# Swapped queries by transfer, the gate with w_ada's columns moving, and other buffer counts in a two-group encoder layer

## The chip, the cores and the metric

The kernel runs on one core of one Trainium2 chip, as one launch. The metric is the device time in microseconds of that core, the median of several executions. Before the change it is 2014.87 us over three runs (2009.33 to 2015.93).

The core has a matrix engine (PE; PEld is its loading of the stationary operand), a vector engine (DVE), a scalar engine for activation functions (ACT), a general engine (POOL), and a queue engine (SP), from which this kernel issues all of its transfers. Every engine and SP work through their own list of instructions in order, and a wait in one holds up what stands behind it in the same list.

## What is computed

One layer of a bidirectional encoder for two groups of 1024 tokens (width 1024), which share all weights. Reduced to what matters here:

```python
mod = silu(c) @ w_ada + b_ada                  # (1024) @ (1024 x 3072)
shift, scale, gate = split(mod, 3)
h = rms_norm(x, norm_g) * (1 + scale) + shift
qa, ka, va, za, qb, kb, vb, zb, ga, gb = split(h @ w_in)
# branch A: 8 query heads, 2 key heads, 64 wide, RMS norm and rotation of q and k
oa = softmax(qa ka^T / 8) va * silu(za)
# branch B: 4 heads, two softmax maps each, 128-wide values
ob = rms_norm((softmax1 - lam * softmax2) vb) * (1 - lam_init) * silu(zb)
merged = sigmoid(ga) * (oa @ w_proj_a) + sigmoid(gb) * (ob @ w_proj_b)
y = x + gate * (merged @ w_out)
```

All data is float32. Most products are made of two halves of each operand, a rounded one (type fp32r) and the remainder, in three matmuls (high x high, high x low, low x high).

## The kernel before

**Tiling.** Everything is cut into 128 partitions. A group's `h` lies transposed in eight large buffers (`u`, 8 KB a partition; pool `upool`, 16 buffers). Keys, queries, values, merged products and the start's inputs use the same pool. Weights come in pieces of 256 columns (`load_w`): four transfers into staging tiles `st` (3 buffers), ACT rounds each (L177), POOL or DVE makes the remainder (L179).

**Queries and keys.** `qa_gen` and `qkb_gen` compute 256 columns for 128 tokens at a time (`proj_tt`, L488). `rms` then takes the mean square (ACT copy and square, DVE sum L504, POOL scaling and addition of EPS L505, POOL power L506), POOL multiplies and rotates (L508 to L528; in the phases where attention does not run, DVE does every second one), PE transposes (L539), and ACT and DVE write the high and low half of a query or key into the two halves of a tile's partitions (L541, L542): high on 0 to 63 and low on 64 to 127, or the other way round.

**Scores.** A unit of attention is one head with 256 queries (two times 128, t = 0 and 1), so 32 units in branch A and 16 in branch B per group; a unit of B has two maps. `softmax_unit` makes 128 x 1024 scores in a PSUM bank `s` (two of them): queries times keys (L697), then the same queries with their partition halves exchanged, `sw`, times the same keys (L698), which gives the four products of the halves in two passes. DVE takes the maximum (L699), ACT the exponential into a tile `p` of probabilities (L700; pool `ppool`, 3 buffers). In B, DVE combines both maps (L733). `flip` transposes on DVE in blocks of 32 (L734) and moves four quarters by transfer into `q`, a tile for the whole unit (L739; two buffers). The values' matmuls then use `q` (L759, L760 in A, L799 in B).

**The swap.** `swapped` copies the halves for 128 queries on POOL, 64 partitions by 128 columns at a time (L565): two instructions for a unit half in A, four in B. It runs one step ahead within a phase: the second half's when the first half's scores are issued, the next unit's when the second half's are. `sw` has two buffers.

**The gate.** `gate_gen` computes the residual's gate for both groups, in group 0's last phase of attention. The stationary operand is a block of w_ada with 128 columns, and the two conditioning vectors move, so a matmul has two columns (L435): 64 matmuls, each a float32 one. At the start, `ada` computes shift and scale the other way round: the two vectors are stationary and 512 columns of w_ada move (L298), and four small transposes turn the row into columns (L307). `inv_rms` (L271) has matmuls that move one column of ones.

**What sets the order.** Streams of generators are woven with shares (`weave`): attention, the making of queries and keys, and the z pieces (`z_gen`, L667; each ends with ACT's copy into the one buffer `ev`, L673, and a store). How many z pieces fall to which phase, and how early each stream runs, is given by the tables at the top (`Z_SHARE`, `ATT_W`, `IN_A` and so on). A scheduler then orders the instructions of each engine, with the attention's at a raised priority. The last phases gate the branches' outputs (`gated_gen`, L895 with a SiLU on ACT), project and merge (`merge_gen`, L940, L951) and project out (`out_gen`, L969).

Of the kernel before, what the change touches and what calls it, by code (L numbers as in the profile page):

```python
# [38 lines left out]
    (7, 18, 4, 3, 5, 6),  # L39
)  # L40
Z_HEAD = (5, 3)
Z_HEAD_A = (-0.35, -0.25)
ATT_W = (
    (1.0, 0.9, 1.1, 0.95, 1.0, 1.322),
    (1.15, 1.265, 0.9, 1.0, 0.85, 1.069),
)
IN_A = (
    (0.1, 0.05, 0.2, 0.05, 0.15, 0.1),
    (0.1, 0.05, 0.45, 0.1, 0.15, 0.55),
# [3 lines left out]
    (0.15, 0.05, 0.35, 0.05, 0.0, -0.1),  # L53
)
LAST_ATT, LAST_FILL = (44, 32)
GATED_A = -0.1
TAIL = 6
TAIL_A = 0.3
LAG = 2

# [28 lines left out]
def kernel(ctx: ExitStack, tc: tile.TileContext, t: dict):  # L89
# [336 lines left out]
    def gate_gen():  # L426
        for n in range(NCH):
            ps = gbank()[:, :2]
            for q in range(2):
                st = spool.tile([P, 4, P], F32, tag="st", name=nm("st"))  # L430
                col = 2 * D + n * P
                dma(st, w_ada[q * 512 : (q + 1) * 512, col : col + P].rearrange("(c p) n -> p c n", p=P))
                for c in range(4):
                    k = q * 4 + c
                    nc.tensor.matmul(ps, st[:, c], cT[:, k], start=(k == 0), stop=(k == NCH - 1))  # L435
            nc.vector.tensor_scalar(out=gatec[:, n], in0=ps, scalar1=bcol[:, 2, n : n + 1], scalar2=None, op0=ALU.add)
            yield 1
# [58 lines left out]
    def rms(ps, nh, e):  # L496
        n = nh * HD
        row = rtile()
        raw, sq = row[:, :n], row[:, 256 : 256 + n]
        nc.scalar.activation(raw, ps, AF.Copy)  # L500
        nc.scalar.activation(sq, raw, AF.Square)
        ss = tiny.tile([P, 4], F32, tag="ss", name=nm("ss"))[:, :nh]
        rs = tiny.tile([P, 4], F32, tag="rs", name=nm("rs"))[:, :nh]
        nc.vector.tensor_reduce(out=ss, in_=sq.rearrange("p (h d) -> p h d", d=HD), axis=AX.X, op=ALU.add)  # L504
        nc.gpsimd.tensor_scalar(out=ss, in0=ss, scalar1=1.0 / HD, scalar2=EPS, op0=ALU.mult, op1=ALU.add)  # L505
# [52 lines left out]
    def swapped(u, qt):  # L558

        qs = u["q"]  # L560
        sw = mtile("sw", [P, 2, P], F32R)[:, : len(qs)]
        sl = slice(qt * P, (qt + 1) * P)
        for m, q in enumerate(qs):
            for a, b in ((LO, HI), (HI, LO)):
                nc.gpsimd.tensor_scalar(  # L565
                    out=sw[a, m], in0=q[b, sl].bitcast(F32), scalar1=1.0, scalar2=1.0, op0=ALU.mult, op1=ALU.mult
                )
        return sw

# [26 lines left out]
    def qa_gen(st, half):  # L596
# [12 lines left out]
        def back(tt, x3):  # L609
            sl = slice(tt * P, (tt + 1) * P)  # L610
            pairs_T(x3, qs[0][:, :, sl], qs[1][:, :, sl])

        yield from pipelined(ht, w, front, back)

    def qkb_gen(ht, out, h):
# [11 lines left out]
        def back(tt, x3):  # L627
            sl = slice(tt * P, (tt + 1) * P)
            pairs_T(x3, qk[0][:, :, sl], qk[1][:, :, sl])

# [25 lines left out]
    def z_gen(ht, col, dst, i0):  # L656
        w = load_w(w_cols(w_in, (col, 256)))
        for hf in range(2):
            for e in range(2):
# [13 lines left out]
                nc.scalar.activation(ev, ps, AF.Copy)  # L673
# [31 lines left out]
    def scores(u, i):  # L705
# [8 lines left out]
        softmax_unit(u["q"][m][:, qt * P : (qt + 1) * P], u["sw"][:, m], u["k"][m], pt, su)  # L714
        if m == 0:
            u[t] = [pt]
            u.pop("next", None)
# [114 lines left out]
    def attention(units):  # L832
# [3 lines left out]
        for n, (ph, make) in enumerate(units):  # L836
# [7 lines left out]
        for at, ph, n, i, qk in steps:  # L844
# [4 lines left out]
            with tc.high_priority(offset=AHEAD):  # L849
# [24 lines left out]
    def gated_gen(st, i, hf, oT):  # L874
# [15 lines left out]
        for c in range(2):  # L890
# [4 lines left out]
            nc.scalar.activation(z, z, AF.Silu)  # L895
# [109 lines left out]
    def units_of(st):  # L1005
# [17 lines left out]

        units = []
        for half in range(2):
            units += [(half, lambda a=(half, i, pr): a_unit(*a)) for i in (0, 2, 1, 3) for pr in range(4)]
        for h in range(4):
            units += [(2 + h, lambda a=(h, pr): b_unit(*a)) for pr in range(4)]
# [9 lines left out]
    def z_item(st, i):  # L1038
        ht = st["ht"]
        if i < 2:  # L1040
            return z_gen(ht, C_ZA + i * 256, st["zd"], i * 2)
        if i < 4:
            return z_gen(ht, C_ZB + (i - 2) * 256, st["zd"], i * 2)
# [118 lines left out]
```

## Time and profile before

| | |
|---|---|
| median of the runs | 2014.87 us |
| the profiled execution | 2017.56 us |
| its span, first to last instruction | 2015.8 us |
| instructions in its records | 31269 |
| transfers' bytes | 278.35 MB, a mean of 138 GB/s |
| transfers of probabilities (q<-p) | 768, each 128 KB, 2.6 us to landing |

The page of the profile gives, in this order: each engine's busy time and share of the span; the span in 40 slices of about 50 us, a digit for each (tenths busy, and in the row PEclk tenths of full clock granted to PE); the transfers' queues; the chain of work that ended last; groups of instructions by line, with total and mean duration and with the idle time ahead of them. In names such as `q<-p` the written tile stands first. A view of waits lists, for each line, how long its engine stood idle before it and whose work ended that. Matmuls overlap in the pipeline, so durations of matmuls add up to more than their stretch.

### The profile page before, as it was taken

The numbers are of one execution on the slowest core, as the hardware profiler recorded it, in microseconds if no ns is written. First come the engines' busy times: TensorE is split into PE (matmuls) and PEld (weight loads), VectorE is DVE, ScalarE is ACT, GpSimd is POOL, SyncE is SP. The second block draws the span as 40 slices with busy tenths as digits, with TensorE's granted clock in tenths as the row PEclk, the third lists the DMA queues.
The fourth block names the chain that finished last, engine by engine and source line by source line (L and its number), as shares of the span: only waits on it lengthen the run. The fifth ranks groups of instructions, "written<-read, shape, count | busy, mean of one in ns | idle before, by whom it ended". The sixth has DMA issues, their size and how long they took to land.

```text
span 2015.8 us, 31269 instructions
## 1 busy us (share of the span) xinstructions
PE 1924.6 (95%) x10554; PEld 1650.9 (82%) x10554; DVE 1305.9 (65%) x1798; ACT 1029.6 (51%) x1956; POOL 963.1 (48%) x1640
## 2 busy tenths in 40 slices
PE   8889999999999999889998899999999999998999
PEld 3778888888978988768888787888887888876887
DVE  4557766776787476546464778667777746664741
ACT  4445655565554345754323556566665434587420
POOL 2475723564677471331235675246577837522210
PEclk9999999999999996999998899999999999999999
DMA  8124545555443327754650345464544323565531
GB/s 306 48 71 109 147 139 137 148 150 154 109 125 95 90 81 206 223 191 160 208 188 32 99 123 152 137 169 126 157 127 126 88 74 90 160 212 192 183 119 73
DMA packets 255199, 278.35 MB, mean 138 GB/s; under 512 B 31680, under 2 KB 205888, under 8 KB 255040
## 3 DMA queue, kind: packets, MB, share of 16 engines
q1 hardware_dynamic: 255040, 276.36, 46.2%
q8 instruction: 84, 1.38, 0.3%
q14 instruction: 75, 0.61, 0.1%
HBM read 133.59 MB, written 42.01 MB: 87 GB/s over the span
## 4 chain that ended last, share of the span: by engine, by line
PE 58%; DVE 10%; DMA 10%; POOL 7%; ACT 6%; issue 5%; SPq 3%; ACTq 0%; POOLq 0%; DVEq 0%
PE f L667 15%; PE f L488 14%; PE f L969 4%; PE s L697 4%; PE s L698 4%; PE s L969 3%; DMA q<-p 3%; PE a L799 3%; DMA p<-zd 2%; PE a L759 2%; PE a L760 2%; SPq L739 2%; DVE m L699 2%; PE f L940 2%; ACT p L700 2%
## 5 line engine op out<-in xcount | busy, mean ns | idle before, releaser
L667 PE MATMUL f<-u,w 128*128 128x512 f32 x2208 | 580.6, 399 | 0.0
L488 PE MATMUL f<-w,u 128*128 128x256 f32 x3456 | 492.2, 288 | 2.8 <-ACT row L500 1.6
L488 PEld LDWEIGHTS f<-w,u 128*128 128x128 f32 x3456 | 464.1, 193 | 24.0 <-ACT row L500 2.7
L667 PEld LDWEIGHTS f<-u,w 128*128 128x128 f32 x2208 | 405.1, 191 | 76.0 <-ACT w L177 0.5
L700 ACT ACTIVATE p<-s,m 128x1024 f32<-128x1024 f32 x256 | 284.7, 1112 | 247.0 <-DMA q<-p 124.6
L699 DVE TENSOR_REDUCE m<-s 128x1 f32<-128x1024 f32 x256 | 310.3, 1217 | 71.6 <-PE s L698 68.2
L179 POOL TENSOR_TENSOR w<-st,w 128x512 fp32r<-128x512 f32 x168 | 231.9, 1396 | 238.7 <-ACT w L177 172.1
L565 POOL TENSOR_SCALAR sw<-u 64x128 fp32r<-64x128 f32 x520 | 180.4, 347 | 307.6 <-PE s L698 264.5
L734 DVE STREAM_TRANSPOSE p<-p 128x1024 f32<-128x1024 f32 x192 | 238.2, 1241 | 114.5 <-ACT p L700 109.2
L748 DVE TENSOR_TENSOR q<-q,hi 128x512 fp32r<-128x512 f32 x256 | 197.4, 790 | 55.0 <-ACT hi L747 53.0
L698 PE MATMUL s<-u,sw 128*128 128x512 f32 x512 | 209.1, 409 | 0.0
L747 ACT ACTIVATE hi<-q 128x512 fp32r<-128x512 f32 x256 | 153.5, 625 | 92.0 <-DMA q<-p 50.0
L177 ACT ACTIVATE w<-st 128x512 fp32r<-128x512 f32 x196 | 113.9, 625 | 93.9 <-DMA st<-in_w_in_dram 39.2
L940 PE MATMUL f<-u,w 128*128 128x512 f32 x564 | 143.5, 405 | 14.3 <-ACT ev L673 7.6
L940 PEld LDWEIGHTS f<-u,w 128*128 128x128 f32 x564 | 107.4, 193 | 39.6 <-DVE u L951 9.2
L759 PE MATMUL a<-hi,u 128*128 128x256 f32 x512 | 131.4, 283 | 5.0 <-DVE oo L776 5.0
L799 PE MATMUL a<-q,u 128*128 128x256 f32 x512 | 132.4, 395 | 1.4 <-issue 1.2
L760 PE MATMUL a<-q,u 128*128 128x256 f32 x512 | 128.6, 285 | 0.6 <-DVE q L748 0.6
L697 PE MATMUL s<-u 128*128 128x512 f32 x256 | 112.4, 440 | 16.5 <-ACT p L700 16.2
L506 POOL TENSOR_TENSOR rs<-ss,nhalf 128x4 f32<-128x4 f32 (+1 forms) x112 | 111.9, 999 | 7.4
L733 DVE SCALAR_TENSOR_TENSOR p<-p,r,p 128x1024 f32<-128x1024 f32 x64 | 91.8, 1434 | 35.2 <-POOL r L721 33.2
L697 PE MATMUL s<-u,u 128*128 128x512 f32 x256 | 104.6, 408 | 10.0 <-ACT p L700 9.7
(176 smaller groups left out, 2713.8 us busy)
## 6 DMA issues: line engine op xcount, KB each, us to landing
q<-p SPq DMA_DIRECT2D x768, 128.0 KB, 2.6
st<-in_w_in_dram SPq DMA_DIRECT2D x132, 256.0 KB, 3.1
zd<-ev SPq DMA_DIRECT2D x96, 256.0 KB, 2.4
p<-zd SPq DMA_DIRECT2D x64, 256.0 KB, 3.1
u<-in_w_ada_dram SPq DMA_DIRECT2D x8, 1024.0 KB, 10.4
st<-in_w_in_dram SPq DMA_DIRECT2D x64, 128.0 KB, 3.1
st<-in_w_out_dram SPq DMA_DIRECT2D x32, 256.0 KB, 3.0
row<-od SPq DMA_DIRECT2D x24, 256.0 KB, 3.3
```

Source lines behind the costliest of these rows:

```text
L179: e.tensor_tensor(out=wl, in0=st, in1=wh.bitcast(F32), op=ALU.subtract)
L488: nc.tensor.matmul(ps, lt[c][:, sl], w[:, c, wi, :], start=(k == 0), stop=(k == 23))
L565: nc.gpsimd.tensor_scalar(out=sw[a, m], in0=q[b, sl].bitcast(F32), scalar1=1.0, scalar2=1.0, op0=ALU.mult, op1=ALU.mult)
L667: nc.tensor.matmul(ps, w[:, c, wi, e * P : (e + 1) * P], rt[c], start=(k == 0), stop=(k == 23),)
L697: nc.tensor.matmul(s[:, sl], q, k[:, sl], start=True, stop=False)
L698: nc.tensor.matmul(s[:, sl], sw, k[:, sl], start=False, stop=True)
L699: nc.vector.tensor_reduce(out=m, in_=s, axis=AX.X, op=ALU.max, negate=True)
L700: nc.scalar.activation(pt.rearrange("p (j c a) -> p j c a", j=4, c=8), s.rearrange("p (c a j) -> p j c a", c=8, j=4), AF.Exp, bias=m, accu ...
L734: nc.vector.transpose(pt, pt)
L748: nc.vector.tensor_tensor(out=tl, in0=tl.bitcast(F32), in1=th.bitcast(F32), op=ALU.subtract)
L799: nc.tensor.matmul(acc, u["v"][:, k], pT[:, k], start=(k == 0), stop=(k == 7))
L940: nc.tensor.matmul(ps, w[:, c, wi, d * P : (d + 1) * P], o[:, oi, :], start=(k == 0), stop=(k == 11))
```

## The change

Five things are changed.

1. `swapped` makes the exchanged halves with two (A) or four (B) transfers of 64 partitions by 256 columns from SP, for the whole unit at once. They are issued behind the flip of the unit's predecessor's first half, if the queries are already there (`made` counts the token tiles that have been written), over a phase's end too; otherwise when the unit begins. `sw` has twice the columns.
2. `gate_gen` is written as `ada` is: the two vectors stationary, 512 columns of w_ada moving, 16 matmuls in place of 64, then eight small transposes.
3. In `rms`, ACT's square takes the factor 1/64 in, and the addition of EPS is DVE's instead of POOL's.
4. The large pool has 15 buffers instead of 16, the probabilities' 4 instead of 3.
5. The tables' numbers are set anew. (The new constant `SILU` is 0, which leaves every SiLU where it was.)

In the built program, PE has 64 matmuls of two columns fewer and 16 of 512 more (and eight transposes), POOL has 520 copies and 112 scalings fewer, DVE 112 additions more, SP 256 transfers more (1502 before, 1758 now), and ACT 41 table loads in place of 58.

```diff
 Z_SHARE = (
     (7, 20, 5, 3, 2, 5),
-    (7, 18, 4, 3, 5, 6),
+    (7, 18, 4, 2, 5, 6),
 )
...
-LAST_ATT, LAST_FILL = (44, 32)
+LAST_ATT, LAST_FILL = (48, 28)
...
-    upool = ent(tc.tile_pool(name="upool", bufs=16))
+    upool = ent(tc.tile_pool(name="upool", bufs=15))
...
-    ppool = ent(tc.tile_pool(name="ppool", bufs=3))
+    ppool = ent(tc.tile_pool(name="ppool", bufs=4))
...
     def gate_gen():
-        for n in range(NCH):
-            ps = gbank()[:, :2]
-            for q in range(2):
-                st = spool.tile([P, 4, P], F32, tag="st", name=nm("st"))
-                col = 2 * D + n * P
-                dma(st, w_ada[q * 512 : (q + 1) * 512, col : col + P].rearrange("(c p) n -> p c n", p=P))
-                for c in range(4):
-                    k = q * 4 + c
-                    nc.tensor.matmul(ps, st[:, c], cT[:, k], start=(k == 0), stop=(k == NCH - 1))
-            nc.vector.tensor_scalar(out=gatec[:, n], in0=ps, scalar1=bcol[:, 2, n : n + 1], scalar2=None, op0=ALU.add)
-            yield 1
+        for half in range(2):
+            acc = gbank()[:2]
+            for k in range(NCH):
+                st = spool.tile([P, 512], F32, tag="st", name=nm("st"))
+                col = 2 * D + half * 512
+                dma(st, w_ada[k * P : (k + 1) * P, col : col + 512])
+                nc.tensor.matmul(acc, cT[:, k], st, start=(k == 0), stop=(k == NCH - 1))
+                if k % 2:
+                    yield 1
+            row = rtile()[:2]
+            nc.vector.tensor_copy(row, acc)
+            ps = gbank()[:, :8].rearrange("p (c g) -> p c g", g=2)
+            for c in range(4):
+                nc.tensor.transpose(ps[:, c, :], row[:, c * P : (c + 1) * P], ident[:2, :2])
...
-        nc.scalar.activation(sq, raw, AF.Square)
+        nc.scalar.activation(sq, raw, AF.Square, scale=1.0 / math.sqrt(HD))
...
-        nc.gpsimd.tensor_scalar(out=ss, in0=ss, scalar1=1.0 / HD, scalar2=EPS, op0=ALU.mult, op1=ALU.add)
+        nc.vector.tensor_scalar(out=ss, in0=ss, scalar1=EPS, scalar2=None, op0=ALU.add)
...
-    def swapped(u, qt):
+    def swapped(u):
 
         qs = u["q"]
-        sw = mtile("sw", [P, 2, P], F32R)[:, : len(qs)]
-        sl = slice(qt * P, (qt + 1) * P)
+        sw = mtile("sw", [P, 2, 256], F32R)[:, : len(qs)]
+        sl = slice(u["pr"] * 256, u["pr"] * 256 + 256)
         for m, q in enumerate(qs):
             for a, b in ((LO, HI), (HI, LO)):
-                nc.gpsimd.tensor_scalar(
-                    out=sw[a, m], in0=q[b, sl].bitcast(F32), scalar1=1.0, scalar2=1.0, op0=ALU.mult, op1=ALU.mult
-                )
+                dma(sw[a, m].bitcast(F32), q[b, sl].bitcast(F32))
         return sw
...
-        if m == 0:
-            u["sw"] = u["next"] if "next" in u else swapped(u, qt)
+        if "sw" not in u:
+            u["sw"] = swapped(u)
...
-                    if t == 0:
-                        late.append(lambda u=live[n]: u.update(next=swapped(u, u["pr"] * 2 + 1)))
-                    elif n + 1 < len(units) and units[n + 1][0] == ph:
+                    if t == (0 if ph < 2 else 0) and n + 1 < len(units) and units[n + 1][2]():
                         live[n + 1] = units[n + 1][1]()
-                        late.append(lambda u=live[n + 1]: u.update(next=swapped(u, u["pr"] * 2)))
+                        late.append(lambda u=live[n + 1]: u.update(sw=swapped(u)))
...
+        def there(kind, n, pr):
+            return made.get(id(st[kind].get(n)), 0) > 2 * pr + 1
```

Three places show how the order moves. The names' numbers tell tiles apart; `x2` at a row's end is a repetition. First POOL, before the change, in branch B, where one head's queries are made while another's scores run: the mean square (L505, L506), multiplications and rotation (L508 to L528), the combining factor (L721), and the swaps (L565).

```order
L565 TENSOR_SCALAR sw_6499<-u_5509 64x128 x2
L565 TENSOR_SCALAR sw_6499<-u_5510 64x128 x2
L721 TENSOR_SCALAR r_6353<-r_6353,suB_118,nlam 128x1
L505 TENSOR_SCALAR ss_6477<-ss_6477 128x4
L506 TENSOR_TENSOR rs_6478<-ss_6477,nhalf 128x4
L508 TENSOR_TENSOR row_6474<-row_6474,rs_6478 128x256
L623 TENSOR_TENSOR row_6474<-row_6474,gB 128x256
L519 TENSOR_TENSOR rc_6484<-row_6474,cosB 128x4x16
L527 TENSOR_TENSOR row_6474<-row_6474,sinB 128x4x8 x2
L565 TENSOR_SCALAR sw_6591<-u_5509 64x128 x2
L565 TENSOR_SCALAR sw_6591<-u_5510 64x128 x2
L528 TENSOR_TENSOR row_6474<-rc_6484,row_6474 128x4x16
```

The same chain on POOL with the change (lines are numbered about ten higher: L515 is the power, L537 the rotation's last step):

```order
L515 TENSOR_TENSOR rs_5550<-ss_5549,nhalf 128x4
L517 TENSOR_TENSOR row_5546<-row_5546,rs_5550 128x256
L634 TENSOR_TENSOR row_5546<-row_5546,gB 128x256
L528 TENSOR_TENSOR rc_5556<-row_5546,cosB 128x4x16
L536 TENSOR_TENSOR row_5546<-row_5546,sinB 128x4x8 x2
L537 TENSOR_TENSOR row_5546<-rc_5556,row_5546 128x4x16
```

The swaps between the steps are gone, and so is the scaling ahead of the power. Second SP with the change, in branch A of group 0: flips (L750), stores of a unit's result (L791) and of a z piece (L688), and the swaps (L574).

```order
L750 DMA q_1996<-p_1954 128x1x256 x4
L791 DMA od_122<-oo_2009 64x256
L750 DMA q_1996<-p_2044 128x1x256 x4
L574 DMA sw_2321<-u_928 64x256 x2
L688 DMA zd_2463<-ev_2461 128x512
L750 DMA q_2108<-p_2085 128x1x256 x4
L750 DMA q_2108<-p_2138 128x1x256 x3
L791 DMA od_123<-oo_2130 64x256
L750 DMA q_2108<-p_2138 128x1x256
L574 DMA sw_2434<-u_928 64x256 x2
```

Two transfers now stand behind each unit's flips. The tile `sw_2321` is for the unit whose flips write `q_2429`; the flips of three other units (`q_2108`, `q_2221`, `q_2316`) stand between. Third PE in group 0's last phase, before the change, at the gate's first matmuls (L435), with scores of branch B (L697, L698) and values (L799):

```order
L435 MATMUL f_8314<-cT,st_8315 128x2 x4
L435 MATMUL f_8314<-cT,st_8321 128x2 x4
L435 MATMUL f_8333<-cT,st_8334 128x2 x4
L697 MATMUL s_8307<-u_7503 128x512
L698 MATMUL s_8307<-u_7503,sw_8300 128x512
L435 MATMUL f_8333<-cT,st_8340 128x2 x4
L697 MATMUL s_8350<-u_7504 128x512
L698 MATMUL s_8350<-u_7504,sw_8300 128x512
L799 MATMUL a_8390<-q_8243,u_7032 128x256 x8
```

And with the change (the gate is L435 again, scores are L709 and L710):

```order
L435 MATMUL f_8152<-st_8167,cT 2x512
L435 MATMUL f_8152<-st_8199,cT 2x512
L435 MATMUL f_8152<-st_8202,cT 2x512
L709 MATMUL s_8208<-u_7420 128x512
L710 MATMUL s_8208<-u_7420,sw_8077 128x512
L709 MATMUL s_8208<-u_7420 128x512
L710 MATMUL s_8208<-u_7420,sw_8077 128x512
L709 MATMUL s_8243<-u_7421 128x512
L710 MATMUL s_8243<-u_7421,sw_8077 128x512
L709 MATMUL s_8243<-u_7421 128x512
L710 MATMUL s_8243<-u_7421,sw_8077 128x512
```

Groups of four matmuls of two columns have become single ones of 512, and four passes of scores stand between two of them.

More of the change, by code (lines that the diff above doesn't have):

```diff
@@ L38 @@
     (7, 20, 5, 3, 2, 5),
-    (7, 18, 4, 3, 5, 6),
+    (7, 18, 4, 2, 5, 6),
 )
-Z_HEAD = (5, 3)
+Z_HEAD = (5, 4)
 Z_HEAD_A = (-0.35, -0.25)
 ATT_W = (
-    (1.0, 0.9, 1.1, 0.95, 1.0, 1.322),
-    (1.15, 1.265, 0.9, 1.0, 0.85, 1.069),
+    (1.0, 0.9, 1.1, 0.95, 1.0, 1.52),
+    (1.229, 1.265, 0.9, 1.0, 0.85, 1.069),
 )
 IN_A = (
-    (0.1, 0.05, 0.2, 0.05, 0.15, 0.1),
-    (0.1, 0.05, 0.45, 0.1, 0.15, 0.55),
+    (0.1, 0.05, 0.4, 0.05, -0.05, 0.1),
+    (0.1, 0.05, 0.4, 0.1, 0.15, 0.55),
 )
@@ L52 @@
     (0.15, 0.0, 0.2, -0.1, 0.0, 0.0),
-    (0.15, 0.05, 0.35, 0.05, 0.0, -0.1),
+    (0.2, 0.05, 0.35, 0.05, 0.0, -0.1),
 )
-LAST_ATT, LAST_FILL = (44, 32)
-GATED_A = -0.1
+LAST_ATT, LAST_FILL = (48, 28)
+GATED_A = -0.2
 TAIL = 6
@@ L59 @@
 LAG = 2
+SILU = 0
 CUTS = (3, 6)
@@ L426, in gate_gen @@
     def gate_gen():
-        for n in range(NCH):
-            ps = gbank()[:, :2]
-            for q in range(2):
-                st = spool.tile([P, 4, P], F32, tag="st", name=nm("st"))
-                col = 2 * D + n * P
-                dma(st, w_ada[q * 512 : (q + 1) * 512, col : col + P].rearrange("(c p) n -> p c n", p=P))
-                for c in range(4):
-                    k = q * 4 + c
-                    nc.tensor.matmul(ps, st[:, c], cT[:, k], start=(k == 0), stop=(k == NCH - 1))
-            nc.vector.tensor_scalar(out=gatec[:, n], in0=ps, scalar1=bcol[:, 2, n : n + 1], scalar2=None, op0=ALU.add)
-            yield 1
+        for half in range(2):
[12 more added lines that the diff above has]
+                nc.tensor.transpose(ps[:, c, :], row[:, c * P : (c + 1) * P], ident[:2, :2])
+            cs = slice(half * 4, half * 4 + 4)
+            nc.vector.tensor_tensor(
+                out=gatec[:, cs], in0=ps, in1=bcol[:, 2, cs].unsqueeze(2).to_broadcast([P, 4, 2]), op=ALU.add
+            )
     def ht_gen(g, ht):
@@ L611, in back @@
             pairs_T(x3, qs[0][:, :, sl], qs[1][:, :, sl])
+            made[id(qs)] = tt + 1
         yield from pipelined(ht, w, front, back)
@@ L629, in back @@
             pairs_T(x3, qk[0][:, :, sl], qk[1][:, :, sl])
+            made[id(qk)] = tt + 1
         yield from pipelined(ht, w, front, back)
@@ L653, in vb_gen, with z_gen @@
             yield 1
-    def z_gen(ht, col, dst, i0):
+    def z_gen(ht, col, dst, i0, fn=AF.Copy):
         w = load_w(w_cols(w_in, (col, 256)))
@@ L709, in scores @@
         qt = u["pr"] * 2 + t
-        if m == 0:
-            u["sw"] = u["next"] if "next" in u else swapped(u, qt)
+        if "sw" not in u:
+            u["sw"] = swapped(u)
         pt = ptile()
         su = u["su"][:, qt : qt + 1] if m == 0 else tiny.tile([P, 1], F32, tag="su", name=nm("su"))
-        softmax_unit(u["q"][m][:, qt * P : (qt + 1) * P], u["sw"][:, m], u["k"][m], pt, su)
+        softmax_unit(u["q"][m][:, qt * P : (qt + 1) * P], u["sw"][:, m, t * P : (t + 1) * P], u["k"][m], pt, su)
         if m == 0:
             u[t] = [pt]
-            u.pop("next", None)
         else:
@@ L835, in attention @@
         steps = []
-        for n, (ph, make) in enumerate(units):
+        for n, (ph, _, _) in enumerate(units):
             na, nv = (2, 4 + PV_LAG) if ph < 2 else (4, 5 + PV_LAG)
@@ L894, in gated_gen @@
             dma(z, st["zd"][(e, hf)])
-            nc.scalar.activation(z, z, AF.Silu)
+            if i >= SILU:
+                nc.scalar.activation(z, z, AF.Silu)
             if e < 4:
@@ L1022, in b_unit @@
             }
+        def there(kind, n, pr):
+            return made.get(id(st[kind].get(n)), 0) > 2 * pr + 1
         units = []
         for half in range(2):
-            units += [(half, lambda a=(half, i, pr): a_unit(*a)) for i in (0, 2, 1, 3) for pr in range(4)]
+            units += [
+                (half, lambda a=(half, i, pr): a_unit(*a), lambda a=("qa", half, pr): there(*a))
+                for i in (0, 2, 1, 3) for pr in range(4)
+            ]
         for h in range(4):
-            units += [(2 + h, lambda a=(h, pr): b_unit(*a)) for pr in range(4)]
+            units += [
+                (2 + h, lambda a=(h, pr): b_unit(*a), lambda a=("qkb", h, pr): there(*a)) for pr in range(4)
+            ]
         return units
```

8 lines of the change are left out of this document (5 added, 3 removed).

## The prediction

> **What bounds the kernel now.** I read the page first, then the granted clock, then who waits for whom, on PE above all, and last the stretch that computes the gate.
>
> ```profile
> span 2015.8 us, 31269 instructions
> ...
> PE 1924.6 (95%) x10554; PEld 1650.9 (82%) x10554; DVE 1305.9 (65%) x1798; ACT 1029.6 (51%) x1956; POOL 963.1 (48%) x1640
> ...
> PEclk9999999999999996999998899999999999999999
> ```
>
> ```profile
> core 0: 2015.8 us, clock 0.974
> ```
>
> PE is busy for 1924.6 of 2015.8 us, so it stands for 91.2 us. A mean clock of 0.974 costs it at most 0.026 x 2015.8 = 52.4 us more. Those two, 144 us, are all that a change without less matrix work can win; the rest is matmuls, and the change leaves all but those of the gate as they are. The digit 6 in the PEclk row (the 16th slice, 756 to 806 us) is the one deep dip. POOL is half idle, so taking work off it wins time only where PE waits for POOL. Who waits, over all engines and then for PE alone and SP's queue:
>
> ```profile
> POOL sw L565 <- PE s L698: 264.5, 67, 14.8
> ...
> ACT p L700 <- DMA q<-p: 124.6, 66, 5.7
> ...
> ACT p L700 <- DVE m L699: 102.5, 67, 6.3
> ```
>
> ```profile
> PE s L697 <- ACT p L700: 25.9, 19, 5.8
> PE f L539 <- POOL row L528: 16.7, 8, 3.5
> PE f L940 <- ACT ev L673: 7.6, 3, 4.3
> ...
> PE f L940 <- DVE u L951: 6.6, 5, 2.7
> ...
> PE s L539 <- POOL row L528: 3.2, 1, 3.2
> ```
>
> ```profile
> SPq L739 <- DVE p L734: 180.7, 42, 14.0
> SPq L201 <- POOL w L179: 141.4, 58, 35.1
> ```
>
> The columns are microseconds in total, times, and the longest. PE's largest wait is for the exponential to free a bank of scores (25.9 us). ACT in its turn waits most for a buffer of probabilities, which comes free when the transfer q<-p has landed (124.6 us). PE's next is for the rotated rows that POOL makes (16.7 + 3.2 us). POOL itself stands 264.5 us at a swap until PE has read the older swapped tile, with the rotation's steps queued behind it.
>
> **The change part by part.** The profiled execution took 2017.56 us (span 2015.8 and 1.8 around it); the sum is made against that. The median of the runs, 2014.87, is 2.7 lower.
>
> *The gate.* Its stretch, and three stretches of the start for comparison:
>
> ```profile
> 28.00:41.00 13.00, 13.00 (x43) 3.49 (x42) 10.63 (x17) 7.70 (x14) 3.44 (x2) 1.00 1.07 373
> 41.00:49.00 8.00, 8.00 (x72) 7.97 (x72) 5.79 (x13) 7.25 (x12) 2.19 (x2) 1.00 0.37 69
> 49.00:56.00 7.00, 7.00 (x28) 6.23 (x28) 2.67 (x8) 0.90 (x3) 2.57 (x3) 0.52 0.50 150
> 754.00:802.00 48.00, 48.00 (x220) 42.56 (x220) 31.86 (x46) 23.76 (x35) 7.91 (x23) 0.68 0.68 198
> ```
>
> ```profile
> 29.90 10.39 PE f L298 x24
> ```
>
> ```profile
> L435 PE MATMUL f<-cT,st 128*128 128x2 f32 x128 | 20.4, 289 | 0.0
> L298 PE MATMUL f<-u,cT 128*2 128x512 f32 x48 | 23.6, 649 | 6.8 <-DMA u<-in_w_ada_dram 6.8
> L271 PE MATMUL f<-ones_c,q 128*128 128x1 f32 x72 | 10.0, 267 | 0.0
> ```
>
> After a stretch's length come busy time (and count) of PE, its weight loads, DVE, ACT and POOL, then the clock. From 754 to 802 us PE is busy in all 48.00 us, yet the mean clock is 0.68: (1 - 0.68) x 48 = 15.4 us are lost. The form explains it: the gate's matmuls load 128 columns and move 2 (L435). At the start the same two forms stand side by side. Matmuls with w_ada moving (L298, 28 to 41 us) hold clock 1.00; then come 72 that move one column (L271, 41 to 49 us), and the next 7 us have 0.52. The new gate is in L298's form, so I take the half clock as gone here. Its matrix time hardly counts: 16 matmuls with two records each (the 64 of before left 128), at 10.39 / 24 = 0.433 us are 13.9 us, against 20.4 us busy before, most of it at the slow clock; eight small transposes come on top. What limits the gain is DVE: 31.86 us of its work lie in those 48 us, in a chain with ACT and PE (maximum, exponential, combination, transposition), so without PE's slowness the stretch cannot end before about 32 us, and not without waits. Bounds 0 and -15.4; I take **-10**, nearer the lost clock.
>
> The Trainium skill weighs against this. Its page "TensorE: Matmul & The Clock Gate", in "Part 1: The HAM clock gate", says that the clock halves after an idle window of about 3.4 us and is restored by sustained activity, and asks only for the absence of idle gaps. By that, a stretch without idle time should not slow down, and changing the matmuls' form would win nothing here. The sum by that rule would be -18 instead of -28. The row with 48.00 of 48 us busy at 0.68 does not fit it.
>
> *Swaps off POOL, and the mean square's last step to DVE.*
>
> ```profile
> L565 POOL TENSOR_SCALAR sw<-u 64x128 fp32r<-64x128 f32 x520 | 180.4, 347 | 307.6 <-PE s L698 264.5 <-issue 9.9 <-PE f L488 1.1
> L505 POOL TENSOR_SCALAR ss<-ss 128x4 f32<-128x4 f32 x96 | 26.2, 273 | 124.7 <-DVE ss L504 120.5 <-DVE ssB L823 0.4
> ```
>
> POOL loses 520 x 0.347 = 180.4 us and at least 26.2 us more, of 963.1. DVE gains 112 small additions; its copy of 128x2 below takes 0.153 us, so about 17 us spread over 2015.8, hidden behind PE, 17 us if nothing covered them. The chain from DVE's sum to POOL's power loses one hop. PE's waits for rotated rows are 16.7 + 3.2 = 19.9 us. Some lie in the heads, where POOL has few swaps in its way; others follow one or two pairs of swaps (0.7 us a pair). Bounds 0 and -19.9; I take **-8**. What is late next there is POOL's split of weights (L179), which stays.
>
> ```profile
> L823 DVE COPY ssB<-f 128x2 f32<-128x2 f32 x32 | 4.9, 153 | 17.0 <-PE f L821 16.8
> ```
>
> *The fourth buffer of probabilities.* One wait as an example, ACT and then PE:
>
> ```profile
> 471.51 1.11 ACT L700 ACTIVATE p<-s,m 128x1024 f32<-128x1024 f32 x1 [5.67 <-DMA q<-p]
> ```
>
> ```profile
> 472.76 0.50 PE L697 MATMUL s<-u,u 128*128 128x512 f32 x1 [0.55 <-ACT p L700]
> ```
>
> ACT stood 5.67 us and PE only 0.55: two score banks and other matmuls cover most of it. Of what ACT waits for at L700, 124.6 us are buffers and 102.5 the maximum, so about half of PE's 25.9 us can be theirs. With a fourth buffer the next wait is the maximum, or the flip's destination. Bounds 0 and -25.9; I take **-8**.
>
> *The large buffers, 16 to 15, and the pieces' new numbers.* No row shows a wait for a large buffer, so the buffers count for zero; if one wait did come, it would be like PE's others, a few microseconds once or twice. The new order has 17 table loads fewer on ACT. What one costs:
>
> ```profile
> 812.58 1.28 ACT L700 ACT_TABLE_LOAD   x1
> ```
>
> ```profile
> 815.14 0.50 PE L697 MATMUL s<-u 128*128 128x512 f32 x1 [2.01 <-ACT p L700]
> ```
>
> Here 1.28 of PE's 2.01 us are the load. Elsewhere ACT is idle half of the time; 17 x 1.28 = 21.8 us are the upper bound, 0 the lower. I take **-3**.
>
> *The clock behind the stalls.* The clock costs 52.4 us in all, 15.4 of them in the gate; of the other 37, stretches follow stalls and narrow matmuls. With a fifth or so of the stalls gone (8 + 8 + 3 of 91.2) I take **-5**; bounds 0 and -37.
>
> *What the transfers add.* The nearest row is the store of 64 partitions with 256 columns, the same size:
>
> ```profile
> L780 SPq DMA_DIRECT2D od<-oo x64: 500/550/613, 175.4 to 1527.0; - x64
> ...
> DMA to landing us min/median/max: 1.9/2.1/3.7
> ```
>
> SP issues 256 more, 0.55 us each: 141 us on a queue that waits 180.7 + 141.4 us at its two costliest places alone, so there is room, but in order. A pair takes 1.1 us to issue and 2.1 to land, 3.2 us, against 0.7 on POOL. In the rows shown above for SP, a swap stands three units' flips ahead of its own unit's, so I count it as landed in time. What is behind it on SP is flips, stores and weight loads, each 1.1 us later (2.2 in branch B), and the buffers of probabilities and of the flips' pairs come free by so much later. A swap too waits on SP until PE has read the tile two units before. Bounds: nothing, and 64 units of A at 1.1 with 32 of B at 2.2, 141 us, if every flip were the last to arrive. PE's share of ACT's waits for flips is some 20% at the most (25.9 of 124.6), which leaves 29. Most flips have slack: I take **+6**, that and the gate's denser scores included.
>
> Sum: -10 - 8 - 8 - 3 - 5 + 6 = **-28**, 2017.6 - 28 = 1989.6 profiled, 1987 as a median.
>
> **The rivals.**
> - *The gate's time does not come back.* The clock in this stretch falls for another reason than the matmuls' form, or DVE takes up the time won. Then the gate's -10 and half of the -5 are gone: about 1999. For it: DVE's 31.86 of 48 us. Against: the three rows of the start. The idle rule of the Trainium skill's page "TensorE: Matmul & The Clock Gate" would give this case; the trace bears it out little.
> - *The stalls go as a whole.* POOL's 19.9, the buffers' half (13), tables 6, the gate's 15, and 12 of the clock behind them, with nothing added: -66, 1949. Against: the waits in the heads have causes that stay.
> - *The waits move.* DVE, busy 65%, becomes what ACT waits for (already 102.5 us), and the ends of the branches keep their waits; only half of the gate's gain is won, 5, and the +6 eats it: 2016. For it: POOL and ACT are off PE's path at most times.
> - *SP's order decides, and the kernel is slower.* If each swap sits ahead of the flip for which ACT's next exponential waits, 29 us are added, the gains from POOL and the buffers are gone, and the gate gives 10: 2014.9 - 10 + 29 = 2034. It decides from where a swap's 1.1 to 2.2 us exceed the slack of a flip, in more than about half of the units. For it: the 66 waits for q<-p. Against: the fourth buffer gives each flip one score unit more.
> - *The swap is not ahead* because the next unit's queries aren't there yet: 3.2 us at a unit's start. That can be so at the first unit of each group, 6 us in all; it changes no case.
>
> **How the numbers follow.** A measurement tells about 0.3% from no change, 6 us here. The forecast (1970 to 2000) has 0.58, the gate's rival (1992 to 2008) 0.14, the large gain (1940 to 1970) 0.11, moved waits (2006 to 2020) 0.10, the slower case 0.07. Faster than 2008.8: the first three and a little of the fourth, 0.85; within 0.3%: 0.08; slower 0.07. The range 1957 to 2011 leaves out about half of the large gain, half of the moved waits and the slower case, under 2 in 10.
>
> **What would show it.** Right: no L565, and no POOL wait on PE; the clock near 1 all through the gate's matmuls, whose stretch is about 38 us long; ACT's wait for q<-p well below 124.6 us; PE's for rotated rows near 12; PE's idle time near 70 us. Wrong: a matmul with sw that waits for a transfer; SP waiting long at the swap's line; the PEclk digit still 6 at the gate; ACT's wait for the maximum grown by what the buffers' fell.

## The result, and the profile after

| | before | after |
|---|---|---|
| median, us | 2013.81 (4 runs, 2009.33 to 2015.93) | 1980.84 (4 runs, 1976.96 to 1987.60) |
| ratio | | 0.9843, 95% interval 0.9811 to 0.9875 |
| profiled execution, us (span) | 2017.56 (2015.8) | 1987.60 (1985.5) |

The median before includes one run more than the three named ahead of the prediction. The kernel is faster by about 32 us (38 to 25 by the interval). First the page after the change: span, busy times, and the row of the granted clock.

```profile
span 1985.5 us, 30670 instructions
...
PE 1908.6 (96%) x10466; PEld 1627.8 (82%) x10466; DVE 1330.8 (67%) x1906; ACT 1009.9 (51%) x1939; POOL 758.1 (38%) x1008
...
PEclk9899999999999999999999999999999999999999
```

```profile
core 0: 1985.5 us, clock 0.982
```

PE stands for 76.9 us instead of 91.2 (14.3 less), and the clock costs 0.018 x 1985.5 = 35.7 us instead of 52.4 (16.7 less). Together that is 31.0 us; the spans differ by 30.3. The deep dip at the gate is gone from the PEclk row. POOL lost 205 us of work and DVE gained 25.

Who waits, for PE, then ACT, then SP's queue (total, times, longest, in us):

```profile
PE s L709 <- ACT p L712: 22.8, 20, 4.0
PE f L548 <- POOL row L537: 7.2, 3, 3.9
...
PE s L548 <- POOL row L537: 5.3, 1, 5.3
PE f L950 <- ACT ev L685: 4.4, 1, 4.4
...
PE f L435 <- DMA st<-in_w_ada_dram: 2.5, 2, 2.1
```

```profile
ACT p L712 <- DVE m L711: 111.3, 73, 6.0
...
ACT p L712 <- DMA q<-p: 84.4, 45, 5.5
```

```profile
SPq L750 <- DVE p L745: 84.2, 37, 10.7
SPq L203 <- POOL w L181: 83.2, 55, 16.6
...
SPq L574 <- ACT row L509: 18.1, 2, 9.0
SPq L574 <- PE s L710: 14.8, 11, 3.9
```

PE's waits for rotated rows (L548) fell from 19.9 us to 12.5. Its wait for the exponential (L709) hardly fell, 25.9 to 22.8, although ACT's wait for buffers of probabilities fell from 124.6 to 84.4. No matmul waits for a swap's transfer. SP waits for the older swapped tile to be read at the swap's line (L574) for only 14.8 us; over all causes it stands there 73.9 us in 52 waits, the longest 9.0 us, so this sign of the prediction is not wholly absent. ACT's wait for the maximum grew by 8.8 us (102.5 to 111.3), while the wait for buffers fell by 40.2. At the gate (L435) there is a new small wait, for w_ada's pieces.

The gate's stretch, from its first matmul to its last transposition (columns as in the prediction: length, then busy time and count of PE, its weight loads, DVE, ACT and POOL, then clock, share of the transfers' engines, GB/s):

```profile
752.60:788.20 35.60, 32.02 (x103) 13.77 (x102) 27.55 (x36) 19.66 (x31) 1.73 (x4) 0.95 0.66 205
```

35.6 us at clock 0.95, where before 48 us ran at 0.68.

By these lines all seems to follow the sum. The experiments show that it does so only as a whole.

### The profile page after: what moved, and what is told of

Same layout as the page of the kernel before. It is cut to its first block, busy times and chain, and to the rows that moved or that the text cites. A ratio compares the mean times of both kernels' runs of the same rounds, so it can differ in the third digit from the quotient of the medians.

```text
span 1985.5 us, 30670 instructions
## 1 busy us (share of the span) xinstructions
PE 1908.6 (96%) x10466; PEld 1627.8 (82%) x10466; DVE 1330.8 (67%) x1906; ACT 1009.9 (51%) x1939; POOL 758.1 (38%) x1008
## 4 chain that ended last, share of the span: by engine, by line
PE 68%; DMA 8%; DVE 8%; ACT 5%; SPq 4%; issue 3%; POOL 3%; ACTq 0%; POOLq 0%; DVEq 0%
PE f L497 16%; PE f L679 16%; PE f L950 6%; PE f L979 5%; PE s L709 4%; PE a L810 4%; PE s L710 4%; PE s L979 4%; DMA q<-p 3%; SPq L750 3%; PE s L950 2%; DVE q L759 2%; PE a L771 2%; PE a L770 2%; DVE m L711 2%
## 5 line engine op out<-in xcount | busy, mean ns | idle before, releaser
L679 PE MATMUL f<-u,w 128*128 128x512 f32 x2232 | 582.3, 398 | 0.1
L497 PE MATMUL f<-w,u 128*128 128x256 f32 x3456 | 487.0, 286 | 2.2 <-ACT ev L685 1.4
L497 PEld LDWEIGHTS f<-w,u 128*128 128x128 f32 x3456 | 459.5, 192 | 22.4 <-ACT ev L685 1.8
L712 ACT ACTIVATE p<-s,m 128x1024 f32<-128x1024 f32 x256 | 284.4, 1111 | 206.3 <-DVE m L711 111.3
L515 POOL TENSOR_TENSOR rs<-ss,nhalf 128x4 f32<-128x4 f32 (+1 forms) x112 | 112.8, 1007 | 322.8 <-DVE ss L514 284.0
L710 PE MATMUL s<-u,sw 128*128 128x512 f32 x512 | 206.7, 404 | 0.0
L950 PE MATMUL f<-u,w 128*128 128x512 f32 x552 | 133.4, 395 | 5.1 <-ACT ev L685 4.4
L709 PE MATMUL s<-u 128*128 128x512 f32 x256 | 110.9, 433 | 15.1 <-ACT p L712 15.1
L810 PEld LDWEIGHTS a<-q,u 128*128 128x128 f32 x512 | 97.8, 196 | 17.5 <-DVE oo L826 1.6
L709 PE MATMUL s<-u,u 128*128 128x512 f32 x256 | 103.6, 405 | 8.3 <-ACT p L712 7.7
L710 PEld LDWEIGHTS s<-u,sw 128*128 128x128 f32 x512 | 98.4, 192 | 15.5
```

The lines of the kernel that those rows point to most:

```text
L497: nc.tensor.matmul(ps, lt[c][:, sl], w[:, c, wi, :], start=(k == 0), stop=(k == 23))
L679: nc.tensor.matmul(ps, w[:, c, wi, e * P : (e + 1) * P], rt[c], start=(k == 0), stop=(k == 23),)
L709: nc.tensor.matmul(s[:, sl], q, k[:, sl], start=True, stop=False)
L710: nc.tensor.matmul(s[:, sl], sw, k[:, sl], start=False, stop=True)
L712: nc.scalar.activation(pt.rearrange("p (j c a) -> p j c a", j=4, c=8), s.rearrange("p (c a j) -> p j c a", c=8, j=4), AF.Exp, bias=m, accu ...
L810: nc.tensor.matmul(acc, u["v"][:, k], pT[:, k], start=(k == 0), stop=(k == 7))
```

## The experiments

Four kernels add one part of the change to the kernel before; five take one part back out of the changed kernel; three keep the gate's part and the order of the rest apart. Ratios are to the kernel before, run beside each kernel on the same chip, with 95% intervals; 0.001 is 2 us. The kernels ran in four sessions, in which the median of the kernel before lay between 2013.8 and 2021.1 us. Where a kernel is compared with one of another session, two ratios are subtracted; the intervals do not cover how much such a ratio may differ from chip to chip.

**1. The gate alone, in the kernel before.** Only `gate_gen` is replaced:

```diff
...
-                    nc.tensor.matmul(ps, st[:, c], cT[:, k], start=(k == 0), stop=(k == NCH - 1))
...
+                nc.tensor.matmul(acc, cT[:, k], st, start=(k == 0), stop=(k == NCH - 1))
...
```

> The kernel before, with the gate's part of the change alone (the two vectors stationary, 512 columns of w_ada moving). My theory: the half clock of the gate's stretch comes from the narrow matmuls' form, so the digit 6 in the clock's row becomes 9, and the time falls by 10 us (between 8 and 15), about 0.5%. Rival A (the clock falls for another reason, or only where PE is idle): the digit stays and the time moves by less than 4 us. Rival B (DVE takes up what is won): the digit goes to 9, but PE's idle time grows by as much, and the time moves by less than 4 us.

Measured 1.0044 (1.0023 to 1.0065), 9 us slower. Up to the gate the kernel is as before (it begins at 755.5 us, before at 754.3), and the gate's stretch did improve, to 44.0 us at clock 0.88. But PE's idle time is 114.3 us instead of 91.2, and 13 of the 23 us more lie in group 1, which has no gate. (These are single executions; the profiled one is 6 us above this kernel's median.) Neither rival speaks of group 1. The built program points to the order: of some 10,100 matmuls and transposes on PE, about half stand at another place in its list than before.

**2. The swaps by transfer alone.** `swapped` and its calls are replaced, and `upool` has 15 buffers, since the larger `sw` needs the room; `ppool` still has 3.

```diff
...
-                nc.gpsimd.tensor_scalar(
-                    out=sw[a, m], in0=q[b, sl].bitcast(F32), scalar1=1.0, scalar2=1.0, op0=ALU.mult, op1=ALU.mult
-                )
+                dma(sw[a, m].bitcast(F32), q[b, sl].bitcast(F32))
...
```

> The kernel before, with the swaps by transfers alone (one tile of 256 columns for each unit, issued ahead), and, since the larger tile takes 2 KB more, 15 large buffers; still 3 buffers of probabilities. My theory: PE's waits for rotated rows fall from 19.9 us to about 12, the swap's transfers delay flips by a few us: the time falls by 4 us (between -10 and +3). Rival A (POOL was never PE's limit outside the heads): within 3 us of before, waits for rotated rows as they were. Rival B (transfers in SP's order stand ahead of flips, and only the fourth buffer of probabilities hides that): slower by 6 to 29 us, with ACT's wait for a flip at the exponential above 124.6 us.

Measured 1.0027 (1.0011 to 1.0044), 5.5 us slower. PE's waits for rotated rows fell as expected (8.7 + 2.8 = 11.5 us, rows below). But new waits came; first PE's rows, then SP's:

```profile
PE f L541 <- POOL row L530: 8.7, 4, 2.8
PE a L803 <- DMA q<-p: 8.1, 3, 4.5
...
PE s L541 <- POOL row L530: 2.8, 1, 2.8
```

```profile
SPq L567 <- PE s L703: 98.4, 49, 10.9
```

SP stands 98.4 us at the swap's line (L567), until PE has read the older `sw`, and the flips stand behind it. PE then waits 8.1 us for flips (L803), which it did nowhere before. So the prediction's rival about SP's order is true here in kind, at a fraction of its price, though not by ACT's wait for flips at the exponential, which is 120.5 us (124.6 before).

**3. Four buffers of probabilities alone** (and 15 large ones).

```diff
-    upool = ent(tc.tile_pool(name="upool", bufs=16))
+    upool = ent(tc.tile_pool(name="upool", bufs=15))
...
-    ppool = ent(tc.tile_pool(name="ppool", bufs=3))
+    ppool = ent(tc.tile_pool(name="ppool", bufs=4))
```

> The kernel before with 4 buffers of probabilities and 15 large ones, and nothing else. My theory: ACT's wait for buffers of probabilities falls from 124.6 us to below 60, PE's for the exponential from 25.9 to about 18, and the time falls by 8 us (between 4 and 14). Rival (the maximum or the flips' destination is late next, so ACT's wait only changes its name): ACT's wait for the maximum grows by what the other fell, and the time moves by less than 3 us.

Measured 1.0023 (1.0007 to 1.0039), 4.6 us slower. ACT's waits:

```profile
ACT p L700 <- DMA q<-p: 119.3, 56, 5.6
ACT p L700 <- DVE m L699: 116.8, 67, 7.9
```

The wait for buffers fell by 5 us only, and that for the maximum grew by 14: the rival's direction, though it does not account for a loss. PE's wait for the exponential rose to 34.5. No run has the 15 large buffers alone, so their part in this loss and in that of experiment 2 is not separated; here too the order differs from before.

**4. The tables alone.** All numbers at the top as in the change, for instance:

```diff
-LAST_ATT, LAST_FILL = (44, 32)
+LAST_ATT, LAST_FILL = (48, 28)
```

> The kernel before with the new numbers of the pieces' tables alone (shares, starts, and the lengths of the last phase). My theory: 17 table loads fewer on ACT and other places of the z pieces, worth 3 us (between 0 and 8). Rival (the retuned tables are the real gain, and the other parts little): faster by 10 us or more. Second rival (the numbers only suit the other parts of the change): 3 us or more slower than before.

Measured 1.0131 (1.0110 to 1.0152), 26 us slower: the second rival. It has 47 table loads on ACT where the kernel before has 58, so fewer loads did not bring the time down. None of these four parts alone, then, makes the kernel before faster, and the numbers alone make it much slower.

**5 to 8. One part taken out of the changed kernel:** the old gate; the swaps on POOL; the old tables; the old mean square. Each is the diff of that part read backwards; the last in full:

```diff
-        nc.scalar.activation(sq, raw, AF.Square, scale=1.0 / math.sqrt(HD))
+        nc.scalar.activation(sq, raw, AF.Square)
...
-        nc.vector.tensor_scalar(out=ss, in0=ss, scalar1=EPS, scalar2=None, op0=ALU.add)
+        nc.gpsimd.tensor_scalar(out=ss, in0=ss, scalar1=1.0 / HD, scalar2=EPS, op0=ALU.mult, op1=ALU.add)
```

> The changed kernel with the gate alone as it was (blocks of w_ada stationary, two columns moving). First theory (each part is worth what its mechanism gives, once the pieces' numbers fit it): the gate's stretch, 35.7 us in the changed kernel, is 48 again with about 15 us lost to the clock, and the time is 10 to 15 us above the changed kernel's (1991 to 1996, ratio to before 0.988 to 0.991). Second theory (the numbers fit this one order, and any edit spoils it): 15 to 35 us above, most of it in group 1, which holds no gate (ratio 0.992 to 1.001).

> The changed kernel with the swaps on POOL again (one half of a unit at a time, as before the change). First theory: PE's waits for rotated rows are 20 us or more instead of 12.5, and the time is 4 to 12 us above the changed kernel's (ratio to before 0.985 to 0.990). Second theory: 15 to 35 us above, with idle time in stretches where PE doesn't wait for POOL. Rival (the transfers cost as much on SP as POOL's work did): within 4 us of the changed kernel.

> The changed kernel with the tables of before (shares, starts, lengths of the last phase). First theory (the parts carry the gain, the numbers are worth 3 us): 2 to 8 us above the changed kernel's time, so 20 us or more below before's (ratio 0.985 to 0.990). Second theory (the numbers are what makes the parts pay): 20 us or more above, so little or nothing is left of the gain (ratio 0.994 to 1.005).

> The changed kernel with the mean square's step as before (POOL scales and adds EPS, 112 instructions of about 0.25 us; ACT's square without a factor). It is nearly neutral by its own work, so it is a yardstick of what a mere shift of the order costs. First theory: 0 to 4 us above the changed kernel (ratio to before 0.983 to 0.987), with the waits for rotated rows up by a few us. Second theory (any edit spoils the order): 8 us or more above.

Measured: old gate 0.9973 (0.9959 to 0.9986), old swaps 0.9974 (0.9959 to 0.9989), old tables 0.9980 (0.9962 to 0.9997), old mean square 0.9823 (0.9799 to 0.9847). Against the changed kernel's 0.9843 that is +26, +26, +28 (each with 7 us either way) and -4 (8 either way). Any one of three parts takes nearly the whole gain with it, which is the second theory's number; with the old gate, group 1 alone is 21.5 us longer in the profiled executions (table below). Yet the fourth contradicts that theory's "any edit": there, too, about half of PE's instructions changed places, and it cost nothing. Orders differ, and some are as good as the changed kernel's. With the old swaps, PE's waits for rotated rows are 16.6 us, 4 more than the changed kernel's 12.5, a small part of the 26:

```profile
PE f L546 <- POOL row L535: 9.8, 4, 3.6
PE s L546 <- POOL row L535: 6.8, 2, 6.0
```

With the old tables the fourth buffer of probabilities did not help ACT either:

```profile
ACT p L712 <- DMA q<-p: 136.0, 60, 6.1
...
ACT p L712 <- DVE m L711: 82.0, 64, 5.3
```

**9. The gate alone, with the order kept.** What couples the gate to everything behind it is a counter:

```python
    def gbank():
        turn[0] += 1
        if alone[0] and turn[0] % 5 in (0, 2):
            return sbank()[:, :512]
        return fbank()
```

In stretches without attention, two of five requests get a bank of scores. The new gate makes 4 requests and the old one 8, so each later choice shifts. One line puts the count where it was:

```diff
                 yield from gate_gen()
+                turn[0] += 4
```

> The gate's part alone in the kernel before, as in the run b_gate, with one line more: the count of bank requests is set forward by 4 behind the gate, since the new gate asks for 4 banks where the old one asked for 8, and by that count modulo 5 every later matmul of the stretches without attention chooses its bank. So each engine's order outside the gate's stretch is nearly that of before. Theory (the gate gives its clock back, and b_gate's loss came from the shifted count and the order that followed): 4 to 10 us below before (ratio 0.995 to 0.998), where b_gate was 9 above, and group 1's stretches within 4 us of before's. Rival (the new gate itself disturbs what follows): as b_gate, 1.002 to 1.006.

Only some 210 of PE's instructions now stand at another place than before: some 60 around the gate, the others within one stretch of about 280 instructions in group 1. Measured 0.9995 (0.9981 to 1.0010): within 0.3% of before, and 10 us (5 either way) better than the gate without that line. So b_gate's loss came from what the count shifts, the order and the choice of banks, as the theory has it; the gate's own gain in time, 4 to 10 us by the theory, did not show. The clock did come back. Its stretch:

```profile
753.30:795.30 42.00, 35.90 (x115) 15.71 (x114) 30.14 (x39) 19.47 (x31) 8.96 (x23) 0.92 0.67 204
```

42 us at 0.92, though PE is busy only 35.90 of them. PE's waits within it:

```profile
PE s L704 <- ACT p L707: 2.1, 1, 2.1
PE f L433 <- DMA st<-in_w_ada_dram: 2.1, 1, 2.1
PE a L806 <- DMA q<-p: 1.7, 2, 1.2
```

The clock lost over the whole kernel, as a median over its runs, is 40.3 us against 52.5 for the kernel before beside it, so 12 us came back. As the time hardly moved, the rest of the span must have grown by about as much. (This kernel's runs lie between 2008 and 2024 us and the profiled one is the fastest, so its stretches look better than its median.)

**10. The changed kernel with the count shifted by 4.** Each instruction is as in the changed kernel; banks and order behind the gate are not, and in most of group 1 the order is that of a_gate_old.

> The changed kernel with one line more: the count of bank requests set forward by 4 behind the gate, which is where it stands with the old gate. Every instruction is that of the changed kernel; from there on only banks and orders differ, and group 1's order is then nearly that of the run a_gate_old. Theory (that run lost some 21 us in group 1 through the order, and the rest through the gate's clock): 12 to 24 us above the changed kernel (ratio to before 0.990 to 0.997). Rival (the old gate itself costs it all): within 5 us of the changed kernel (0.982 to 0.987).

Measured 0.9900 (0.9885 to 0.9915), 11.5 us slower (7 either way), at the lower edge of the theory's 0.990 to 0.997 and above the rival's 0.982 to 0.987: order and banks alone, without one instruction more or less. PE's waits in the whole kernel:

```profile
PE s L709 <- ACT p L712: 33.5, 23, 4.9
PE f L548 <- POOL row L537: 8.6, 6, 2.3
```

The wait for the exponential is 10.7 us longer, most of it in group 1.

**11. The old gate in the changed kernel, with the count put right.**

```diff
                 yield from gate_gen()
+                turn[0] += 1
```

> The changed kernel with the old gate, as in a_gate_old, and the count of bank requests set forward by 1 behind it, so that the stretches without attention choose the banks of the changed kernel. Theory (gate and order are two separate costs): the gate's stretch is 48 us again, and the time is 8 to 15 us above the changed kernel's instead of 26 (ratio to before 0.988 to 0.992); group 1's order is like the changed kernel's in the stretches without attention, not in branch A, so a further 5 us either way are possible. Rival (the old gate costs it all): as a_gate_old, 0.996 to 0.999.

Measured 0.9855 (0.9836 to 0.9874): 2.4 us above the changed kernel, with 7.5 either way, and 24 us below a_gate_old, from which it differs by that line. That is less than the 8 to 15 us above the changed kernel that the theory had. The order is not wholly the changed kernel's: about a fifth of PE's instructions, nearly all in group 1, stand at another place. Its gate:

```profile
744.30:793.40 49.10, 47.19 (x200) 42.26 (x199) 28.88 (x41) 23.59 (x37) 2.97 (x6) 0.62 0.63 185
```

49.1 us at 0.62, 13.5 us longer than the new gate's stretch.

**12. Three buffers of probabilities in the changed kernel.**

> The changed kernel with 3 buffers of probabilities instead of 4 (15 large ones, as there is no room for 16). First theory (the fourth buffer is worth 8 us through PE's wait for the exponential): ACT's wait for buffers of probabilities is back above 110 us from 84.4, PE's for the exponential up from 22.8 to about 30, and the time 4 to 12 us above the changed kernel (ratio to before 0.986 to 0.991). Second theory (only the order counts): the wait for buffers may grow, but the time moves by what the order gives, anything from 0 to 28 us, with PE's wait for the exponential no guide to it. Rival (the transfers' delays are what the fourth buffer hides): 12 us or more above, with PE waits for flips or swaps.

Measured 0.9912 (0.9899 to 0.9926), 14 us above the changed kernel (7 either way). ACT's first row, SP's at the swap, and PE's:

```profile
ACT p L712 <- DMA q<-p: 122.0, 65, 5.6
```

```profile
SPq L574 <- PE s L710: 68.8, 38, 6.0
```

```profile
PE s L709 <- ACT p L712: 24.0, 16, 3.7
...
PE a L810 <- DMA q<-p: 4.3, 3, 2.0
...
PE a L770 <- DMA q<-p: 4.2, 1, 4.2
```

PE's wait for the exponential is nearly as in the changed kernel, so the fourth buffer does not pay where I had put it. What is back is SP's wait at the swap (68.8 us for 14.8) and PE's wait for flips (8.5 us, where the changed kernel has 0.4). In experiment 2 the swaps by transfer had the same two marks with three buffers. The first goes with three buffers: at the swap's line SP waits for PE's reading of the older tile 98.4 and 68.8 us with three, and 14.8 to 31.1 us in the six kernels that have four and swaps by transfer. The second does not: PE waits for flips 5.2 us in b_tables and 5.8 us in b_gate, both with the swaps on POOL, and 5.6 us in a_rms_old, which has four buffers and is no slower than the changed kernel. About half of PE's list stands at other places than in the changed kernel as well. So that swaps by transfer need the fourth buffer is likely, but how many of the 14 us are due to that is not shown.

All profiled executions side by side, one for each kernel. "Idle" is PE's, "clock" is the span times (1 - granted clock, unrounded), "rest" is the span less both. "Group 0" runs from the first scores to group 0's first matmul of the output projection, "group 1" from there to the end (with group 0's projection).

| kernel | ratio | idle | clock | rest | group 0 | group 1 |
|---|---|---|---|---|---|---|
| before | 1 | 91.2 | 53.1 | 1871.5 | 816.7 | 1057.2 |
| b_gate | 1.0044 | 114.3 | 48.6 | 1872.7 | 817.3 | 1075.2 |
| b_gate_turn | 0.9995 | 95.5 | 37.5 | 1873.3 | 810.2 | 1053.1 |
| b_swap | 1.0027 | 98.6 | 62.0 | 1868.2 | 817.6 | 1068.4 |
| b_bufs | 1.0023 | 98.3 | 55.5 | 1867.1 | 819.2 | 1059.6 |
| b_tables | 1.0131 | 114.8 | 61.9 | 1867.2 | 822.6 | 1079.3 |
| after | 0.9843 | 76.9 | 35.8 | 1872.8 | 789.9 | 1046.2 |
| a_turn | 0.9900 | 92.2 | 34.8 | 1875.1 | 791.6 | 1063.2 |
| a_gate_old | 0.9973 | 88.1 | 54.6 | 1871.4 | 805.0 | 1067.7 |
| a_gate_old_turn | 0.9855 | 70.7 | 47.8 | 1867.7 | 801.8 | 1043.1 |
| a_swap_old | 0.9974 | 99.3 | 39.3 | 1869.6 | 805.8 | 1060.3 |
| a_bufs_old | 0.9912 | 92.5 | 38.2 | 1870.7 | 802.5 | 1055.5 |
| a_tables_old | 0.9980 | 94.2 | 39.3 | 1874.3 | 796.2 | 1070.3 |
| a_rms_old | 0.9823 | 77.1 | 27.3 | 1875.4 | 798.6 | 1040.0 |

The rest is 1867 to 1875 us in all fourteen, while the spans differ by up to 64 us. So beyond some 8 us, the differences in time are PE's idle time and its clock.

## Why the prediction was right, and where its steps were not

**The total and its two halves held.** The prediction had -28 us, and the profiled executions differ by 30. Its terms for the clock, -10 and -5, make 15; 16.7 was measured. Of that, the gate's stretch gives 13.6 (15.4 lost before, 0.05 x 35.6 = 1.8 after), while the start lost some 6 us more than before's in this one execution (0.09 x 149.4 against 0.05 x 141.9). Its terms for the stalls, -8 - 8 - 3 + 6, make 13; 14.3 was measured. The opening argument, that idle time and clock are all that can be won, is borne out by the table's constant rest. What it said would show the steps right came true: no L565, the gate at clock 0.95 in 35.6 us (38 predicted), rotated rows 12.5 us (12), PE's idle time 76.9 (70).

**The gate, -10: the mechanism is shown, the size depends on what follows.** With the old form the stretch runs at 0.62 to 0.68 (three profiles), with the new one at 0.88 to 0.95 (four). Between kernels whose order behind the gate is the same or largely the same, the clock lost over the whole kernel, as medians over the runs, falls by 12 us (before and b_gate_turn), 13 (a_gate_old_turn and after) and 19 (a_gate_old and a_turn); in the second pair the orders still differ in part (experiment 11). In time, the same exchange is worth 1 us (4 to -2) in the kernel before, 2.4 (10 to -5) in the changed one, and 14.7 (11 to 19) in the order of a_turn against a_gate_old. My reason for taking less than the whole 15.4, that the stretch becomes limited by what works beside PE, was right in kind. In experiment 9 the waits are for w_ada's transfers, the exponential and flips, not for DVE's busy time alone; and the rival "the gate's time does not come back" is what happened there.

The rule of the Trainium skill's page "TensorE: Matmul & The Clock Gate", "Part 1: The HAM clock gate", that the clock halves after an idle window, does not fit these rows either, as far as the records' busy time tells when PE is idle: with the old gate PE is busy for 47.19 of 49.10 us at 0.62, with the new one for 35.90 of 42.00 at 0.92. More idle time, less clock lost.

**The swaps, -8 with +6 for what the transfers add: not terms of their own.** The expected relief at the rotated rows is there (11.5 us in experiment 2, 12.5 in the changed kernel). But alone the swaps cost 5.5 us, and taken out they cost 26. The working said that SP has room and that the tile two units before would be read in time. With three buffers of probabilities it was not: SP waited 98.4 and 68.8 us there. With four it is 14.8.

**The fourth buffer, -8: a gain of 14 when the rest is there, and not by the path named.** I had it act through PE's wait for the exponential; that is 22.8 with four buffers and 24.0 with three. The runs point to the swap's queue instead, though they do not show that it costs PE the 14 us (experiment 12).

**The tables, -3: the step that failed.** I counted 17 table loads and called the rest of the retuning zero. The numbers cost 26 us in the kernel they were not made for, and leaving them out costs 28 in the one they were. In the first case there are 11 table loads fewer than before and in the second 8 more than in the changed kernel (49 against 41); 28 us are more than 8 loads can cost at 1.28 us each. What else the numbers do is place the z pieces among this program's other streams, which a count of instructions cannot show; that the 26 and 28 us come from there is inferred.

**The assumption under the sum failed with it:** that the parts add. Taken out singly they are worth 2 (the gate, order put right) + 26 + 14 + 28 = 70 us. Put in singly, the gate with its order kept gains 1 us, and the other three lose 5, 5 and 26. Together they are worth 32. That the sum came out so near was luck: its bound, the 144 us that PE loses in all, leaves room for many other results, and its terms do not hold one by one.

**What stays open.** Why one order is 10 to 25 us better than another is not traced to one wait. In a_turn PE's longer wait for the exponential is 10.7 of the 15.3 us of idle time more; the rest is spread over many places. That every part could pay alone with numbers set for it was not tried. Stretches in the table are of single executions, and these differ by some microseconds without any edit. The start, up to the first scores, took 149.4 us at clock 0.91 in the profiled run of the changed kernel and 141.4 us at 0.95 in that of a_gate_old, whose program is the same up to the gate; in that of a_turn it took 147.3, in all others 141 to 144.

## What to carry to other kernels

Where an engine is 95% busy, bound the whole by its idle time and its lost clock, and trust that bound more than a split of it over the edits. Before crediting or blaming a part, ask what it shifts by the way (a counter, a rotation of banks, a scheduler's order), and run it once more with that put back: one line moved the same old gate from 2013 to 1989 us. Numbers that place work are fitted to one program, so a part added without setting them anew can measure as a loss though its mechanism works.

## What the runs showed of the hardware

The clock of a stretch followed the matmuls' form, not PE's busy share. These are the gate's matmuls in both forms, first of a_gate_old_turn, then of the changed kernel (line, tiles, stationary operand, moving operand, count, busy time, mean ns):

```profile
L437 PE MATMUL f<-cT,st 128*128 128x2 f32 x128 | 23.8, 311 | 0.0
```

```profile
L435 PE MATMUL f<-st,cT 128*2 128x512 f32 x32 | 15.7, 609 | 2.5 <-DMA st<-in_w_ada_dram 2.5
```

128 matmuls of two columns at a mean of 311 ns left PE no gap ahead of them (0.0 us) and ran in a stretch at 0.62; 32 of 512 columns waited 2.5 us for their data and ran in one at 0.95.
